# Moving the adaLN products of a two-layer diffusion backbone from TensorE to GpSimd

## The chip, the cores and the metric

One core of a Trainium2 chip runs the whole forward pass. The metric is device time of one execution in microseconds, as the median of several runs. The engines are TensorE (PE in the rows, PEld for its weight loads), VectorE (DVE), ScalarE (ACT), GpSimd (POOL) and SyncE (SP), which only issues DMAs. Each engine takes its own instructions in order and waits on semaphores for the others.

## The reference

Two layers, 256 latent tokens and 256 context tokens of width 1024 in float32. Each layer first turns a conditioning vector into six modulation vectors of 1024 (adaLN):

```python
mod_x = [m[:, None, :] for m in jnp.split(silu_c @ ada_w[i] + ada_b[i], 6, axis=-1)]
mod_c = jnp.split(silu_cc @ ada_w[i] + ada_b[i], 6, axis=-1)
hx = _modulate(_rms(x, norm1_w[i]), mod_x[0], mod_x[1])
y_x, y_c = _mixer(hx @ w_in[i], hc @ w_in[i], ...)
x = x + mod_x[2] * (y_x @ w_out[i])
x = x + mod_x[5] * ffn(_modulate(_rms(x, norm2_w[i]), mod_x[3], mod_x[4]))
```

`mod_x` (one column, from `c`) is for the latent tokens and `mod_c` (a second column, from `c_ctx`) for the context. Vectors 0 and 1 are shift and scale ahead of the mixer, 2 is the gate behind it, 3 and 4 are shift and scale ahead of the FFN, 5 is its gate. The mixer is an mLSTM with attention beside it; the FFN is a dense SwiGLU in layer 0 and eight experts with two chosen per token in layer 1. Layer 1 updates no context behind its mixer, so its vectors 2 to 5 need one column only.

## The kernel before

The weights of the dense products stream through `raw` tiles of 128x1024. Each is split into a high and a low float32r part (ScalarE line 143, VectorE line 144), and `mm3` (lines 328 to 331) makes one product of three matmuls. `gemm` (335) runs units of 128 output columns over 8 or 11 contraction tiles and yields after each unit. `mixer` (382) weaves four generators by a small clock (`STEPS`, line 39): the projections that are left, the mLSTM heads, the attention, and `extra`, the adaLN work. `ffn` (822) is a generator of four `gemm` calls. `bridge` (796) runs the end of a projection into the norm and the start of the next stage. At the end come the router and `experts`, whose weights are prefetched by SP into 16 buffers.

The adaLN products are made by `ada` (187). One part is two of the six vectors, 8 MB of weights in eight steps of 1 MB. For the first part of layer 0 this runs ahead of the first mixer, and this part stays as it is. The other five parts run through `adas` (228) as `extra` of a mixer: (0,1), (0,2) and (1,0) in mixer 0; (1,1) and (1,2) in mixer 1. One step loads two tiles `araw` of 512 KB by SP and makes eight matmuls `ada` with 32 columns of `cz` as weights (line 208; `cz` holds the SiLU of both conditioning vectors); after eight steps `sums` copies the row out, transposes it (217), and VectorE adds up four groups and the bias (220, 222).

Emission sets what each engine is given, but the framework reorders instructions within an engine when it builds the program, by its own estimates of when operands are ready. A pool's tile with one buffer makes the next writer wait for the last reader.

POOL has little to do: it clears `kz`, `akz` and `va` at the start of each mixer (417 to 422), clears `qkv` and `qkr` in `qk_norm` (642 to 655), multiplies the query and key tiles by the cosine table (678), clears `zb` (978), and issues two DMAs (962, 1285). In layer 1 `g2p` (970) spreads the gate of vector 5 over the partitions, for the experts; it stands among the products of the output projection.

Of the kernel before, what the change touches and what calls it, by code (L numbers as in the profile page):

```python
# [9 lines left out]
F32 = mybir.dt.float32  # L10
# [4 lines left out]
ALU = mybir.AluOpType  # L15
# [4 lines left out]
KT = 8  # L20
# [4 lines left out]
FCUT = 24  # L25
FE = 3584
NE = 8
BIG = 1e30
NRAW = 2
NWH = 5  # L30
UB = 4
EB = 2
# [13 lines left out]
HEAD = 3  # L46
# [3 lines left out]
TAILD = 3  # L50
# [18 lines left out]
def tile_hybrid(ctx: ExitStack, tc, a, tap=None):  # L69
# [155 lines left out]

        return load, products, sums

    def adas(pool, *parts):
        todo = [(*f, k) for f in [ada(l, p, pool, "araw", 2, 2) for l, p in parts] for k in range(KT)]
        todo[0][0](0)  # L230
        for i, (_, products, sums, k) in enumerate(todo):
            if k == 0:
                o = ps("ax", name="ada")
            products(o, k, k, k == 0, k == KT - 1)
            if i + 1 < len(todo):
                todo[i + 1][0](todo[i + 1][3])
            yield
            if k == KT - 1:
                sums(o, range(KT))
                yield  # L240

    def mod(layer, i, j):

# [138 lines left out]
    def mixer(layer, pool, extra):  # L382
# [253 lines left out]
        def qk_norm():  # L636

            dve.tensor_scalar(qwl, qw[:, layer:layer + 1], 0.125, None, op0=ALU.mult)
            w = PA.tile([128, TOK], F32, tag="sc", name="qkv", bufs=4)
            if not full:  # L640
                act.activation(w[0:32, 0:256], ssq[0][0:32, 0:256], AF.Copy)
                nc.gpsimd.memset(w[32:64, 0:256], 0.0)
                nc.gpsimd.memset(w[64:128, 0:256], 0.0)
            act.activation(w[:, q0:], ssq[0][:, q0:], AF.Copy)
            pt = ps("ax", name="qkT")
            for t in range(4):
                pe.transpose(pt[:, t * 128:(t + 1) * 128], w[:, t * 128:(t + 1) * 128], ident)
            v = tile("qv", [128, 64])
            r = tile("qr", [128, 64])
            view = lambda z: z.rearrange("p (t g r) -> p t g r", t=4, g=4)  # L650
            dve.tensor_scalar(view(v), view(pt)[:, :, :, 0:4], 1.0 / 64, EPS, op0=ALU.mult, op1=ALU.add)
            rsqrt(M, v, r, "q")
            yield
            w2 = PA.tile([128, TOK], F32, tag="sc", name="qkr", bufs=4)
            nc.gpsimd.memset(w2, 0.0)
            dve.tensor_copy(view(w2)[:, :, :, 0:4], view(r))
            pt = ps("ax", name="qkr")
            for t in range(4):
                pe.transpose(pt[:, t * 128:(t + 1) * 128], w2[:, t * 128:(t + 1) * 128], ident)
            rh = PA.tile([128, TOK], F32R, tag="sc", name="rh", bufs=4)  # L660
            rl = PA.tile([128, TOK], F32R, tag="sc", name="rl", bufs=4)
            act.activation(rh, pt, AF.Copy)
            dve.tensor_sub(rl, pt, rh)
            rot = cs[:, C_ROT - 128:C_ROT - 128 + 128]
            yield
            for i in (4, 0, 1, 2, 3):
                lo = 0 if i == 4 else q0
                b = ps("ax", name="qb")
                pe.matmul(b[:, lo:], qsel[:, i, :], rh[:, lo:], start=True, stop=False)
                pe.matmul(b[:, lo:], qsel[:, i, :], rl[:, lo:], start=False, stop=True)  # L670
                wc = kw[:, layer:layer + 1] if i == 4 else qwl
                z = qa[i]
                dve.scalar_tensor_tensor(z[:, lo:], z[:, lo:], wc, b[:, lo:], op0=ALU.mult, op1=ALU.mult)
                rp = ps("ax", name="rp")
                pe.matmul(rp[:, 0:256], rot, z[:, 256:512], start=True, stop=True)
                u = PA.tile([128, TOK], F32, tag="sc", name="u", bufs=4)
                dve.tensor_mul(u[:, 0:256], rp[:, 0:256], cs[:, C_SIN - 128:C_SIN - 128 + 256])
                nc.gpsimd.tensor_mul(u[:, 256:512], z[:, 256:512], cs[:, C_COS - 128:C_COS - 128 + 256])
                if i == 4:
                    for hv in range(2):  # L680
                        rr = slice(64 * hv, 64 * hv + 64)
                        dve.tensor_add(akz[hv][rr, 256:512], u[rr, 0:256], u[rr, 256:512])
                        act.activation(akz[hv][rr, 0:256], z[rr, 0:256], AF.Copy)
                else:
                    dve.tensor_add(z[:, 256:512], u[:, 0:256], u[:, 256:512])
                yield
# [135 lines left out]
    def ffn(acc):  # L822
        with tc.tile_pool(name="ff", bufs=1, reuse_waits="tile") as FF:
            f_rhs = [[], []]
            hold = {}

            def evac(key, o, *_):
                kind, m = key
                if kind == "g":
                    s = PA.tile([128, TOK], F32, tag="sc", name="sg", bufs=4)  # L830
                    act.activation(s, o, AF.Silu)
                    hold[m] = s
                    return
                f = PA.tile([128, TOK], F32, tag="sc", name="f", bufs=4)
                dve.tensor_mul(f, o, hold.pop(m))
                H = FF.tile([128, TOK], F32R, tag="fh", name="fh", bufs=15)
                L = FF.tile([128, TOK], F32R, tag="fl", name="fl", bufs=15)
                act.activation(H, f, AF.Copy)
                dve.tensor_sub(L, f, H)
                f_rhs[m // 11].append((H, L))  # L840

            def evac_d(key, o, lo, hi):
                half, m = key
                add_gated(0, 5, m, o, lo, hi)
                if half == 1:
                    if m == 0:
                        acc.append(new_acc())
                    square_add(acc[0], m, lo, hi)

            gu = [(0, (n, m)) for m in range(NFF) for n in ("g", "u")]  # L850
            down = lambda i: [(0, (i, m)) for m in range(KT)]
            yield from gemm(gu[:FCUT], hp, evac, KT, head=HEAD, halves=True)
            yield from gemm(down(0), f_rhs[0], evac_d, 11)
            yield from gemm(gu[FCUT:], hp, evac, KT)
            yield from gemm(down(1), f_rhs[1], evac_d, 11, head=HEAD, tail=TAILD)


    a0, mx = ExitStack(), ExitStack()
# [21 lines left out]
    S = Stats(acc)  # L880
    S.sums(0, TOK)
    M0 = mixer_pool("mix0", a0)
    g = mixer(0, M0, adas(lambda: mx.pool, (0, 1), (0, 2), (1, 0)))
    A = new_coef()
    def products0(k):
        o = ps("ax", name="ada")
# [27 lines left out]
    g = ffn(acc2)  # L914
    bridge(p, TAIL, acc, 0, 1, g)

    p, g = g, mixer(1, mixer_pool("mix1"), adas(lambda: mx.pool, (1, 1), (1, 2)))
    bridge(p, TAILD, acc2, 1, 0, g)
    run(g)
    mx.close()  # L920
# [444 lines left out]
def layout(i):  # L1365
# [10 lines left out]
    for h in range(4):  # L1376
# [9 lines left out]
    o["consts"] = np.ascontiguousarray(c[:, 128:])  # L1386
    o["ada"] = np.ascontiguousarray(i["ada_w"].reshape(2, 8, 128, 3, 2, 8, 128).transpose(0, 3, 5, 2, 1, 4, 6)
                                    ).reshape(2, 3, 8, 128, 2048)
    un = _units()
    win = np.zeros((2, 1024, NU * 128), np.float32)  # L1390
    for n, u in enumerate(UNITS):
# [43 lines left out]
```

## Time and profile before

| | |
|---|---|
| median of 3 runs | 1835.87 us (1835.19 to 1839.09) |
| the profiled execution | 1834.92 us, span of its trace 1833.2 us |
| mean granted TensorE clock | 0.988 of full |
| TensorE busy | 1724.5 us, 94% |
| VectorE busy | 586.9 us, 32% |
| ScalarE busy | 443.8 us, 24% |
| GpSimd busy | 19.6 us, 1% |
| HBM read | 469.36 MB, 257 GB/s over the span |

The stages, read off the lines at work: mixer 0 with its projections up to about 317 us, the FFN to about 700, mixer 1 and its output projection to 900, the router to 940, the experts to the end. A row of the profile names the line of the kernel, the engine, the operation, and the tiles as output<-input. float32 matmuls appear as two records each, float32r ones as one. "Idle before" is the time in which the engine had nothing to run ahead of that instruction, with what ended it. Matmul ends are modelled, so the durations of neighbours overlap; the step from start to start is the better measure.

### The profile page before, as it was taken

What the parts mean: (1) busy time and instruction counts of PE and PEld (TensorE: products, weight loads), DVE (VectorE), ACT (ScalarE), POOL (GpSimd) and SP (SyncE); (2) the same over time, 40 slices, a digit from 0 to 9 for tenths busy, and PEclk for the clock granted to TensorE, in tenths of its full rate; (3) what the DMA queues carried; (4) which work ended last, traced back from release to release, by engine and by line L of the source; (5) the groups of instructions that cost most, each with busy time, mean ns of one, the idle gap of its engine ahead of it and who ended that gap; (6) DMA issues with size and microseconds to landing.
All of it is one profiled execution on the core that took longest, in us unless ns stands there. A gap on an engine that the chain in (4) does not pass through costs nothing. (4 is left out here: it accounts for less than half of the span.)

```text
span 1833.2 us, 30457 instructions
## 1 busy us (share of the span) xinstructions
PE 1724.5 (94%) x13016; PEld 976.3 (53%) x13016; DVE 586.9 (32%) x1341; ACT 443.8 (24%) x852; POOL 19.6 (1%) x43
## 2 busy tenths in 40 slices
PE   6999899999999999999979999998988899999995
PEld 4866458888888889765734333333322233333331
DVE  6635565633333348465410200202020200211103
ACT  4543553432122225544311000101001000000001
POOL 1001000000000000000000000000000000000000
PEclk9999999999999999999989999999999999999997
DMA  8435541333333324465869999999999999999970
GB/s 314 148 122 182 181 160 58 99 97 95 101 92 93 103 70 137 140 196 160 326 255 417 416 418 399 361 417 416 418 416 417 417 416 418 403 408 357 339 305 24
DMA packets 84856, 472.65 MB, mean 258 GB/s; under 512 B 9424, under 2 KB 9808, under 8 KB 69088
## 3 DMA queue, kind: packets, MB, share of 16 engines
q1 hardware_dynamic: 84240, 469.36, 67.0%
q8 instruction: 118, 1.93, 0.4%
q0 software_dynamic: 176, 0.56, 0.1%
q10 hardware_dynamic: 288, 0.52, 0.1%
q14 instruction: 34, 0.28, 0.0%
HBM read 469.36 MB, written 1.05 MB: 257 GB/s over the span
## 5 line engine op out<-in xcount | busy, mean ns | idle before, releaser
L1145 PE MATMUL up<-rawe,G 128*32 128x448 f32 x5120 | 509.7, 543 | 19.0 <-PEq L1129 7.2
L1145 PEld LDWEIGHTS up<-rawe,G 128*32 128x32 f32 x5120 | 165.4, 110 | 339.0 <-issue 292.3
L329 PE MATMUL mm<-hh,wh 128*128 128x512 f32 (+1 forms) x856 | 305.4, 360 | 4.2 <-ACT hh L324 4.0
L330 PE MATMUL mm<-hl,wh 128*128 128x512 f32 (+1 forms) x856 | 304.4, 356 | 0.0
L331 PE MATMUL mm<-hh,wl 128*128 128x512 f32 (+1 forms) x856 | 303.4, 355 | 0.0
L1170 PE MATMUL y<-rawe,e 128*32 128x512 f32 x2240 | 252.4, 594 | 6.6 <-DMA rawe<-in_md_dram 3.3
L143 ACT ACTIVATE wh<-raw 128x1024 fp32r<-128x1024 f32 x120 | 127.1, 1059 | 329.8 <-PE mm L330 293.6
L144 DVE TENSOR_TENSOR wl<-raw,wh 128x1024 fp32r<-128x1024 f32 x120 | 146.7, 1223 | 176.9 <-ACT wh L143 174.4
L329 PEld LDWEIGHTS mm<-hh,wh 128*128 128x128 f32 x856 | 161.0, 189 | 31.1 <-ACT hh L324 5.4
L330 PEld LDWEIGHTS mm<-hl,wh 128*128 128x128 f32 x856 | 161.8, 189 | 27.3 <-issue 5.2
L331 PEld LDWEIGHTS mm<-hh,wl 128*128 128x128 f32 x856 | 161.7, 189 | 23.6 <-issue 1.6
L1210 DVE TENSOR_TENSOR hid<-sg,up 128x448 f32<-128x448 f32 x48 | 27.1, 617 | 424.7 <-PE up L1145 424.7
L1170 PEld LDWEIGHTS y<-rawe,e 128*32 128x32 f32 x2240 | 72.6, 109 | 162.9 <-issue 148.5
L1102 DVE TENSOR_TENSOR ye<-y,yc 32x512 f32<-32x512 f32 x48 | 32.7, 682 | 202.5 <-ACT yc L1100 201.8
L1191 ACT ACTIVATE e<-hT 128x384 f32<-128x384 f32 x48 | 23.4, 490 | 290.3 <-PE hT L1190 289.7
L329 PE MATMUL mm<-fh,wh 128*128 128x512 f32 (+1 forms) x209 | 75.3, 360 | 0.0
L330 PE MATMUL mm<-fl,wh 128*128 128x512 f32 (+1 forms) x209 | 75.1, 359 | 0.0
L331 PE MATMUL mm<-fh,wl 128*128 128x512 f32 (+1 forms) x209 | 75.1, 359 | 0.0
L1206 ACT ACTIVATE sg<-up 128x448 f32<-128x448 f32 x48 | 22.8, 544 | 209.5 <-PE up L1145 209.5
L208 PE MATMUL ada<-araw,cz 128*32 128x256 f32 x640 | 54.2, 390 | 13.6 <-DMA araw<-in_ada_dram 13.4
L1100 ACT ACTIVATE yc<-y 64x512 f32<-64x512 f32 x24 | 14.2, 593 | 207.6 <-PE y L1170 202.5
L330 PEld LDWEIGHTS mm<-fl,wh 128*128 128x128 f32 x209 | 39.3, 188 | 6.6
(265 smaller groups left out, 1362.5 us busy)
## 6 DMA issues: line engine op xcount, KB each, us to landing
rawe<-in_mg_dram SPq DMA_DIRECT2D x128, 896.0 KB, 17.5
rawe<-in_mu_dram SPq DMA_DIRECT2D x128, 896.0 KB, 17.3
rawe<-in_md_dram SPq DMA_DIRECT2D x112, 1024.0 KB, 17.0
raw<-in_ws_dram SPq DMA_DIRECT2D x120, 512.0 KB, 3.6
araw<-in_ada_dram SPq DMA_DIRECT2D x80, 512.0 KB, 4.4
a<-in_ada_dram SPq DMA_DIRECT2D x8, 1024.0 KB, 11.6
xall<-in_xT_dram SPq DMA_DIRECT2D x2, 1024.0 KB, 6.3
fn<-in_fn_dram POOLq DMA_DIRECT2D x1, 512.0 KB, 5.1
```

Of the source, the lines that this page charges most:

```text
L143: act.activation(h, raw, AF.Copy)
L144: dve.tensor_sub(l, raw, h)
L208: pe.matmul(o[32 * g:32 * g + 32, 0:256], cz[:, kt, 16 - 2 * row:48 - 2 * row], t[:, z:z + 256], start=(first and kt < 4), stop=(last and ...
L329: pe.matmul(out, wh, hh, start=first, stop=False)
L330: pe.matmul(out, wh, hl, start=False, stop=False)
L331: pe.matmul(out, wl, hh, start=False, stop=last)
L1102: dve.tensor_add(ye[32 * s:32 * s + 32, n * 512:(n + 1) * 512], y[s][32 * n:32 * n + 32, :], yc[32 * n:32 * n + 32, :])
L1145: pe.matmul(o[s][32 * c:32 * c + 32, 0:SC], g[:, k, 32 * s:32 * s + 32], w[k][:, c * SC:(c + 1) * SC], start=(k == 0), stop=(k == KT - 1), ...
L1170: pe.matmul(y[s][r:r + 32, :], e[s][:, 2 * i + par, :], w[i - lo][:, par * 1024 + n * 512:par * 1024 + (n + 1) * 512], start=(i == 0), sto ...
L1191: act.activation(e[s][:, 12 * st:12 * st + 12, :], pt[:, 0:384].rearrange("p (q c) -> p q c", c=32), AF.Copy)
L1206: act.activation(sg[s], o[:, 0:SC], AF.Silu)
L1210: dve.tensor_mul(hid[st, s], sg[s], o[:, 0:SC])
```

## The change

All vectors but the first two of layer 0 are now made on GpSimd. For each half of a vector (512 outputs) POOL itself issues eight DMAs of 256 KB, from the weights in a new layout `adb`. For each of the eight tiles it multiplies by one value of `cz` per partition and adds into an accumulator `au0` or `au1`, once for each column that is needed. TensorE then sums each accumulator over the partitions with a vector of ones, four matmuls of 128x1 per accumulator. VectorE adds the bias. Vectors (0,2) to (0,4) run beside mixer 0; (0,5), (1,0) and (1,1) beside the FFN, one step after each yield; (1,2) to (1,5), one column each, beside mixer 1. The weight tiles `araw` have two buffers in the mixers and four in the FFN; the accumulators and `af` have one each. The cosine multiplication goes from POOL to VectorE.

```diff
+EXTRA = 1
...
-    def adas(pool, *parts):
-        todo = [(*f, k) for f in [ada(l, p, pool, "araw", 2, 2) for l, p in parts] for k in range(KT)]
-        todo[0][0](0)
-        for i, (_, products, sums, k) in enumerate(todo):
-            if k == 0:
-                o = ps("ax", name="ada")
-            products(o, k, k, k == 0, k == KT - 1)
-            if i + 1 < len(todo):
-                todo[i + 1][0](todo[i + 1][3])
-            yield
-            if k == KT - 1:
-                sums(o, range(KT))
-                yield
+    def adas(pool, bufs, *vectors):
...
+        for layer, i in vectors:
+            nj = 1 if layer and i > 1 else 2
+            if (layer, i // 2) not in mods:
+                mods[layer, i // 2] = P1.tile([128, 16, 2], F32, name=f"mod{layer}{i // 2}")
+            for n in range(2):
+                z = slice(i % 2 * 8 + 4 * n, i % 2 * 8 + 4 * n + 4)
+                u = [pool().tile([128, 512], F32, tag=f"au{j}", name=f"au{j}", bufs=1) for j in range(nj)]
+                for k in range(KT):
+                    t = pool().tile([128, 512], F32, tag="araw", name="araw", bufs=bufs)
+                    nc.gpsimd.dma_start(t, a["adb"][layer, i, n, k])
+                    for j in reversed(range(nj)):
+                        c = cz[:, k, 16 + j:17 + j]
+                        if k == 0:
+                            nc.gpsimd.tensor_scalar(u[j], t, c, None, op0=ALU.mult)
+                            continue
+                        f = pool().tile([128, 512], F32, tag="af", name="af", bufs=1) if j else t
+                        nc.gpsimd.tensor_scalar(f, t, c, None, op0=ALU.mult)
+                        nc.gpsimd.tensor_tensor(u[j], u[j], f, ALU.add)
+                    if k % 2:
+                        yield
+                o = ps("ax", name="adas")
+                for j in range(nj):
+                    for k in range(4):
+                        pe.matmul(o[:, k * nj + j:k * nj + j + 1], u[j][:, k * 128:(k + 1) * 128], ones,
+                                  start=True, stop=True)
+                bias = adab[:, layer, i // 2 * 16 + z.start:i // 2 * 16 + z.stop]
+                dve.tensor_add(mods[layer, i // 2][:, z, 0:nj], o[:, 0:4 * nj].rearrange("p (k j) -> p k j", j=nj),
+                               bias.unsqueeze(2).to_broadcast([128, 4, nj]))
...
-                nc.gpsimd.tensor_mul(u[:, 256:512], z[:, 256:512], cs[:, C_COS - 128:C_COS - 128 + 256])
+                dve.tensor_mul(u[:, 256:512], z[:, 256:512], cs[:, C_COS - 128:C_COS - 128 + 256])
...
-            yield from gemm(gu[:FCUT], hp, evac, KT, head=HEAD, halves=True)
-            yield from gemm(down(0), f_rhs[0], evac_d, 11)
-            yield from gemm(gu[FCUT:], hp, evac, KT)
-            yield from gemm(down(1), f_rhs[1], evac_d, 11, head=HEAD, tail=TAILD)
+            extra = adas(lambda: FF, 4, (0, 5), (1, 0), (1, 1))
+            for g in (gemm(gu[:FCUT], hp, evac, KT, head=HEAD, halves=True), gemm(down(0), f_rhs[0], evac_d, 11),
+                      gemm(gu[FCUT:], hp, evac, KT), gemm(down(1), f_rhs[1], evac_d, 11, head=HEAD, tail=TAILD)):
+                for mark in g:
+                    if mark == "tail":
+                        run(extra)
+                    yield mark
+                    step(extra, EXTRA)
...
-    g = mixer(0, M0, adas(lambda: mx.pool, (0, 1), (0, 2), (1, 0)))
+    g = mixer(0, M0, adas(lambda: mx.pool, 2, (0, 2), (0, 3), (0, 4)))
...
-    p, g = g, mixer(1, mixer_pool("mix1"), adas(lambda: mx.pool, (1, 1), (1, 2)))
+    p, g = g, mixer(1, mixer_pool("mix1"), adas(lambda: mx.pool, 2, *((1, i) for i in range(2, 6))))
```

The order of the instructions shows where the new work stands. Lines of the changed kernel are 20 to 24 higher than before in the same code (329 is 349, 970 is 994).

TensorE in the FFN, in a unit of the gate and up products. `mm` is the unit's output, `hh`/`hl` the high and low tokens, `wh`/`wl` the high and low weights. Before:

```order
L329 MATMUL mm<-hh_89,wh 128x512 [waits DVE_49]
L330 MATMUL mm<-hl_90,wh 128x512
L331 MATMUL mm<-hh_89,wl 128x512
L329 MATMUL mm<-hh_91,wh 128x512
L330 MATMUL mm<-hl_92,wh 128x512
L331 MATMUL mm<-hh_91,wl 128x512
```

And in the change, at the third of the six sums in the FFN:

```order
L349 MATMUL mm<-hh_91,wh 128x512
L350 MATMUL mm<-hl_92,wh 128x512
L351 MATMUL mm<-hh_91,wl 128x512
L256 MATMUL adas<-ones,au_3328 128x1 [waits Pool_49]
L256 MATMUL adas<-ones,au_3328 128x1 x3
L256 MATMUL adas<-ones,au_3329 128x1 x4
L349 MATMUL mm<-hh_93,wh 128x512
L350 MATMUL mm<-hl_94,wh 128x512
L351 MATMUL mm<-hh_93,wl 128x512
```

Eight sums now stand inside the unit, the first with a wait for POOL; the next such place is 85 products further on.

POOL at the same time, from one half-vector to the next. Before, POOL had nothing in the FFN; its neighbours there were the last cosine product of mixer 0 and the first memsets of mixer 1:

```order
L678 TENSOR_TENSOR u<-qa_510,cs 128x256 [waits DVE_49,Pool_49]
L678 TENSOR_TENSOR u<-qa_511,cs 128x256 [waits DVE_49,Pool_49]
L417 MEMSET kz_5745 64x512 [waits DVE_49,PE_49,Pool_49]
L417 MEMSET kz_5746 64x512
L417 MEMSET kz_5747 64x512
```

In the change (`au_3329` and `au_3328` are the accumulators of one half-vector, `au_3430` and `au_3429` those of the next):

```order
L249 TENSOR_SCALAR af<-araw,cz 128x512 [waits DMASW2_49,Pool_49]
L250 TENSOR_TENSOR au_3328<-au_3328,araw 128x512 [waits Pool_49]
L249 TENSOR_SCALAR araw<-araw,cz 128x512 [waits Pool_49]
L246 TENSOR_SCALAR au_3430<-araw,cz 128x512 [waits DMASW1_49,PE_49]
L246 TENSOR_SCALAR au_3429<-araw,cz 128x512 [waits Pool_49]
L250 TENSOR_TENSOR au_3430<-au_3430,af 128x512 [waits Pool_49]
L250 TENSOR_TENSOR au_3429<-au_3429,araw 128x512 [waits Pool_49]
L242 DMA araw<-in_adb_dram 128x512 x3
```

The product that opens the new accumulator waits for TensorE, which has to have read the old one; the last add of the old half-vector and two products of the new one's second tile stand in front of it.

TensorE at the end of mixer 1's output projection. Before, the router's sum of squares `ss` followed the last product at once, and `g2p` stood further up among the products:

```order
L329 MATMUL mm<-hh_103,wh 128x256
L330 MATMUL mm<-hl_104,wh 128x256
L331 MATMUL mm<-hh_103,wl 128x256
L286 MATMUL ss<-ones,acc 128x1 [waits DVE_49,PE_49]
L286 MATMUL ss<-ones,acc 128x1
```

In the change (`au_7786`, `au_7824` and `au_7862` are the last three half-vectors, of (1,4) and (1,5)):

```order
L351 MATMUL mm<-hh_103,wl 128x256
L256 MATMUL adas<-ones,au_7786 128x1 [waits PE_49,Pool_49]
L256 MATMUL adas<-ones,au_7786 128x1 x3
L256 MATMUL adas<-ones,au_7824 128x1 [waits PE_49,Pool_49]
L256 MATMUL adas<-ones,au_7824 128x1 x3
L256 MATMUL adas<-ones,au_7862 128x1 [waits PE_49,Pool_49]
L256 MATMUL adas<-ones,au_7862 128x1 x3
L994 MATMUL g2p<-sml,mod_7685 128x128 [waits DVE_49]
L994 MATMUL g2p<-sml,mod_7685 128x128 x3
L994 MATMUL g2p<-sml,mod_7685 128x128 [waits DVE_49]
L994 MATMUL g2p<-sml,mod_7685 128x128 x3
L306 MATMUL ss<-ones,acc 128x1 [waits PE_49]
```

Three sums with a wait for POOL and all of `g2p` now stand between the last product and the router.

## Rows read from the trace of the kernel before

**Rows 1.** The page, part 1: busy time, share of the span, instructions.

```profile
PE 1724.5 (94%) x13016; PEld 976.3 (53%) x13016; DVE 586.9 (32%) x1341; ACT 443.8 (24%) x852; POOL 19.6 (1%) x43
```

**Rows 2.** Windows by stage: length, busy time of each engine, granted clock, DMA, GB/s.

```profile
core 0: us, PE busy (x) PEld busy (x) DVE busy (x) ACT busy (x) POOL busy (x), PEclk, DMA share, GB/s
...
144.00:262.00 118.00, 112.04 (x738) 64.13 (x737) 71.39 (x228) 60.18 (x172) 4.96 (x5) 1.00 0.55 180
...
317.00:700.00 383.00, 380.84 (x1890) 321.91 (x1889) 156.33 (x248) 114.74 (x152) 3.26 (x10) 1.00 0.31 95
...
784.00:880.00 96.00, 89.41 (x635) 57.43 (x634) 57.97 (x191) 47.49 (x114) 4.31 (x6) 0.98 0.51 162
...
900.00:940.00 40.00, 28.65 (x192) 16.76 (x194) 13.12 (x58) 9.30 (x21) 0.58 (x1) 0.83 0.55 213
940.00:1833.00 893.00, 831.05 (x7852) 294.02 (x7844) 125.60 (x228) 79.58 (x151) 0.00 (x0) 0.98 0.94 379
```

**Rows 3.** The page, part 5: the products that the change removes.

```profile
L208 PE MATMUL ada<-araw,cz 128*32 128x256 f32 x640 | 54.2, 390 | 13.6 <-DMA araw<-in_ada_dram 13.4
```

**Rows 4.** POOL by line, shapes apart: busy us, mean ns; its last memset by time.

```profile
L678 POOL TENSOR_TENSOR u<-qa,cs 128x256 f32<-128x256 f32 x8 | 6.4, 797 | 19.3 <-DVE qa L673 10.8 <-DVE rd L607 3.6 <-DVE mod L222 2.7
...
L678 POOL TENSOR_TENSOR u<-ka,cs 128x256 f32<-128x256 f32 x2 | 2.4, 1180 | 63.0 <-DVE ka L673 63.0
...
L655 POOL MEMSET qkr<- 128x512 f32 x2 | 1.1, 527 | 96.0 <-PE ssq L470 91.0 <-ACT E L576 5.0
L962 POOL DMA_DIRECT2D wr<-in_router_dram x1 | 0.7, 697 | 0.8 <-POOLq L1425 0.8
L1285 POOL DMA_DIRECT2D fn<-in_fn_dram x1 | 0.6, 580 | 35.9 <-PE tT L1021 35.9
...
L422 POOL MEMSET va<- 128x4 f32 x8 | 0.4, 98 | 0.0
...
L976 POOL COPY wr<-wr 128x64 f32<-128x64 f32 x1 | 0.2, 237 | 4.7 <-DMA wr<-in_router_dram 4.7
...
41.41 0.20 POOL L422 MEMSET va<- 128x4 f32 x4
```

**Rows 5.** Line 678 alone: duration in ns, least, median and most.

```profile
L678 POOL TENSOR_TENSOR u<-qa,cs x8: 726/750/1148, 169.5 to 820.1; 128x256 f32<-128x256 f32 x8
```

**Rows 6.** Timeline of TensorE's weight loads at a 128x1 product: start us, us.

```profile
317.48 0.53 PEld L286 LDWEIGHTS ss<-ones,acc 128*128 128x128 f32 x4
...
317.93 0.19 PEld L329 LDWEIGHTS mm<-hh,wh 128*128 128x128 f32 x1
```

**Rows 7.** Timeline of TensorE: the products next to which the sums now stand.

```profile
144.24 0.39 PE L569 MATMUL U<-mask,identb 128*128 128x512 bf16 x1
...
262.17 1.12 PE L709 MATMUL sc<-akz,qa 128*128 128x512 f32 x2
...
331.74 0.28 PE L331 MATMUL mm<-hh,wl 128*128 128x256 f32 x1
...
425.19 0.39 PE L329 MATMUL mm<-hh,wh 128*128 128x512 f32 x1
...
784.40 0.39 PE L331 MATMUL mm<-hh,wl 128*128 128x512 f32 x1
...
900.21 0.28 PE L331 MATMUL mm<-hh,wl 128*128 128x256 f32 x1
```

**Rows 8.** Windows of the removed products (`ada`) alone: length, PE busy.

```profile
100.00:144.00 44.00, 6.33 (x64) 1.92 (x64) 0.00 (x0) 0.00 (x0) 1.00 0.43 144
...
262.00:275.00 13.00, 2.16 (x32) 0.47 (x24) 0.48 (x2) 0.39 (x1) 1.00 0.25 82
700.00:784.00 84.00, 4.26 (x56) 1.20 (x56) 0.00 (x0) 0.00 (x0) 1.00 0.43 141
```

**Rows 9.** DMA issues by POOL: KB each, median us from issue to landing.

```profile
fn<-in_fn_dram POOLq DMA_DIRECT2D x1, 512.0 KB, 5.1
...
wr<-in_router_dram POOLq DMA_DIRECT2D x1, 32.0 KB, 5.6
```

More of the change, by code (lines that the diff above doesn't have):

```diff
@@ L1388, in layout @@
                                     ).reshape(2, 3, 8, 128, 2048)
+    o["adb"] = np.ascontiguousarray(i["ada_w"].reshape(2, 8, 128, 6, 2, 512).transpose(0, 3, 4, 1, 2, 5))
+    o["ada"] = np.ascontiguousarray(o["ada"][:1, :1])
     un = _units()
```

## The prediction

> **What bounds the kernel now.** I read the page's shares first. TensorE is busy 94% of the span and GpSimd (POOL) 1% [rows 1], so moving work from the one to the other looks free. The stage windows say where a change can act [rows 2]. From 940 us on the expert weights stream at 379 GB/s with the DMA engines 94% busy; nothing there is touched. Between 900 and 940 us, while routing is worked out, they are only 55% busy: their buffers are full and wait for TensorE. So whatever moves the start of the experts, early or late, moves the end by as much. In the FFN TensorE is busy 380.8 of 383 us, in the two mixers 112.0 of 118 and 89.4 of 96. What the change takes out is one group: 54.2 us busy, with 13.6 us idle in front of it, in which the weights were still on their way [rows 3]; together 67.8 us, or 1.25 us for each busy one. POOL today runs a few instructions [rows 4]. I read them last, and they decide.
>
> **What TensorE saves.** It loses the 67.8 us. It gains the sums: 12 two-column half-vectors of 8 matmuls and 8 one-column ones of 4, 128 matmuls, each two records: 256. The nearest row is `ss`, the same shape: 4 records take the weight path from 317.48 to 317.93, 0.113 us each [rows 6]. That is 1.8 us for a two-column half-vector, 0.9 for a one-column one, 29 us in all. TensorE's saving is at most 67.8 - 29 = 39 us, if it never waits.
>
> **What POOL gets.** A two-column half-vector issues 8 DMAs, 16 TENSOR_SCALARs and 14 TENSOR_TENSOR adds, all 128x512; a one-column one 8, 8 and 7. None stands in the trace at this size, so each is bounded.
> - DMA issue: 0.697 and 0.580 us [rows 4]. I take 0.64.
> - TENSOR_SCALAR: not under MEMSET 128x512, 0.527, which reads nothing. Above, by COPY: 237 ns for 64 elements, less the 98 ns of the smallest MEMSET, is 2.17 ns each, so 1.21 us for 512. I take 0.75, nearer to the row of the right size.
> - TENSOR_TENSOR: 128x256 takes 726 ns at least, 750 in the median [rows 5]. Doubling all but a fixed 237 ns (a whole COPY) gives 1.22 us from the least, doubling all but 98 ns gives 1.40 from the median. I take 1.33. In the mixers the ten of them mean 874 ns [rows 4], 1.165 times the median, because VectorE is busy beside them: 1.55 there, at most 1.63.
>
> The accumulators have one buffer, so the first product of a half-vector waits until TensorE has summed the one before, as POOL's order shows. POOL and TensorE therefore run in a cycle: POOL's work, then the sums. I add 1.8 us for these and 1.0 for waits of POOL on its own results (0.9 and 0.5 for one column), which no row shows. **One cycle**: FFN 16 x 0.75 + 14 x 1.33 + 8 x 0.64 + 2.8 = 38.5 us (30.9 to 47.4); mixer 0 the same with 1.55, 41.6 us (30.9 to 50.6); mixer 1 8 x 0.75 + 7 x 1.55 + 8 x 0.64 + 1.4 = 23.4 us (18.2 to 28.1). The low ends take the shortest rows and half of the sums as covered.
>
> The Trainium skill speaks against this change (GPSIMD Engine Reference, section 4.1): elementwise work belongs on VectorE, and two-input operations are about twice as slow on GpSimd. Its section 3.1 times an add of 2048 elements at 4497 ns; a quarter, 1.12 us, as an estimate by that page, would make the FFN's cycle 35.6 us and its term below 85 instead of 99. No run here shows that size.
>
> **What waits.** TensorE takes its instructions in order. A sum that POOL hasn't finished holds back every product behind it: projections, scores, FFN. Idle POOL time elsewhere is worth nothing; what counts is how far apart the sums stand. I place them by the product in front of each, in the trace of before [rows 7].
> - *Mixer 0.* The first sum stands behind the mask product at 144.24, which ends by 144.6. Of that, 6.33 us busy since 100 us are products that go [rows 8], with their idle 7.9, so TensorE arrives at 137. POOL can start behind the memsets at about 41.6 us [rows 4] and has long finished; but then it waits for this sum. Five cycles later, at 137 + 208 = 345, comes the sixth sum. TensorE stood at that place, among the last score products, at 262. That is +83, less 2.7 for the products removed after 262 [rows 8]: **+80 us** (+26 to +125).
> - *FFN.* First and sixth sum stand at 331.74 and 425.19, 93.5 us apart, 18.7 a cycle. The first I cost at nothing: 67 us lie between it and the mixer's last sum, and one POOL pass needs 36; if the FFN's buffers came free over 30 us late, it would show. Five cycles of 38.5 take 192.5: **+99 us** (+61 to +144). Nothing can be won back, TensorE being full on either side.
> - *Mixer 1.* The first sum stands at 784.40, less 4.26 x 1.25: 779. Seven cycles later is 943. The last three sums stand behind the whole output projection, whose last product started at 900.21: **+42 us** (+6 to +76).
> - *Behind it* the eight `g2p` products, which stood inside the projection, now wait for the last sum: 16 records, **+2 us**.
>
> Costed at nothing: VectorE's ten rope multiplications, at most 0.8 us each by POOL's rows and beside the waits above; the removed row copies and reductions; SP, rid of 80 issues with none behind them that is late; POOL's own memsets for `qkr` and `qkv`, now queued behind products, since they come before the sum that holds TensorE anyway. If POOL were fast these memsets would be next to show, because query and key normalisation wait for them. TensorE's clock fell to a granted 0.83 in the stage with waits [rows 2]; a lower level inside a cycle would be hidden, as TensorE needs half of it.
>
> **Sum**: 80 + 99 + 42 + 2 = +223 us. The profiled execution took 1834.9 us (span 1833.2), 1.0 below the median of 1835.87: 1834.9 + 223 = **2058 us**. Low ends together: +95, 1930 us. High ends together: +346, 2181 us; that all four prices are at their high end is unlikely, so I stop at 2140.
>
> **The rivals.**
> - *Faster: POOL keeps up and TensorE never waits.* The point is in the FFN: a cycle under 18.7 us. Then the saving on TensorE is whole, and the time 1835 - 39 = 1796. For it: POOL is idle 99% of the span, and the order places the sums as if about 19 us were enough. Against it: 38 instructions in 18.7 us is 0.49 each, under even the MEMSET's 0.527, while an add of half the size takes 0.726. Chance 0.04.
> - *Prices mostly fixed per instruction.* If 128x512 adds cost 0.80, little more than 128x256, and products 0.527, a two-column cycle is 25 us. Then mixer 0 loses nothing, the FFN 33 us, and mixer 1 gains up to 14, for it is TensorE's again: 1835 + 20, so 1815 to 1930. For it: MEMSET 128x4 at 98 ns says no, COPY at 237 ns for 64 elements says perhaps. Chance 0.10, of which 0.02 within 0.2%.
> - *POOL and VectorE block each other, or the loads come late.* `ka`'s multiplication took 1180 ns in the mean against 797 for `qa` [rows 4]. If every add were so stretched, 2.1 us, a two-column cycle would be 49 us, with the one-column at 27: 1835 + 117 + 152 + 68 + 2 = 2174. In mixer 1 there are two load buffers; POOL's two DMAs landed after 5.6 and 5.1 us [rows 9], and a round of landing, product and add, 5.3 + 2.3, covers two tiles: 3.8 us a tile against 2.9 by POOL's work, 51 us more over seven cycles. Chance 0.10. The Trainium skill (SBUF — State Buffer, section "Who interferes with whom") says that a VectorE instruction with two SBUF inputs and a GpSimd one that reads SBUF exclude each other for whole instructions; the stretched rows agree with it.
> - *The change does less than it says.* TensorE's 54.2 us could hardly shrink if the sums were dear; at 0.113 us a record they are not. Folded into the forecast.
>
> **How the numbers follow.** My forecast, a POOL-paced kernel between 1930 and 2140, has 0.76; above it 0.10, below it 0.14 in two cases. Range 1930 to 2140, nearly 8 in 10. About 0.2% (3.7 us) is what a measurement of this kernel tells from no change: faster 0.04, same 0.02, slower 0.94.
>
> **What would show it.** POOL busy for some 500 us (256 products x 0.75 and 224 adds x 1.4); the idle time before the sums' line on TensorE, released by POOL, of 180 us or more; sums in the FFN 38 us apart instead of 19; the expert stage as long as before and some 220 us later. A POOL add near 0.8 us, or sums without idle time before them, would make the forecast wrong; so would idle time that VectorE or a DMA ends instead.

## The result and the profile after

The changed kernel takes **2282.03 us** (median of four runs, 2276.1 to 2282.66) against 1835.53 us before: a ratio of 1.2426, 95% interval 1.2399 to 1.2453. The forecast was 2058 us, 1930 to 2140. The direction and the mechanism held, the size did not: the rise is 447 us where 223 were forecast. The profiled execution has a span of 2280.7 us, 447.5 more than before.

Busy times of the page, where [rows 1] had 19.6 us for POOL:

```profile
PE 1773.1 (78%) x12622; PEld 1045.4 (46%) x12622; DVE 658.8 (29%) x1361; ACT 439.4 (19%) x845; POOL 824.6 (36%) x673
```

Windows by stage, columns as in [rows 2]:

```profile
139.00:262.00 123.00, 68.82 (x310) 50.45 (x309) 49.67 (x127) 32.90 (x88) 104.57 (x83) 0.76 0.20 58
262.00:400.00 138.00, 50.75 (x226) 33.88 (x226) 41.78 (x109) 26.74 (x83) 125.62 (x101) 0.67 0.14 40
500.00:745.00 245.00, 110.63 (x461) 92.49 (x461) 42.15 (x43) 28.29 (x37) 228.69 (x177) 0.69 0.23 73
500.00:800.00 300.00, 165.63 (x695) 138.08 (x696) 59.63 (x66) 41.77 (x53) 230.44 (x180) 0.74 0.24 75
800.00:1115.00 315.00, 306.77 (x1596) 259.87 (x1595) 144.83 (x240) 106.71 (x160) 38.70 (x35) 0.99 0.32 101
1115.00:1345.00 230.00, 112.53 (x632) 88.44 (x630) 81.09 (x216) 47.79 (x118) 186.38 (x159) 0.72 0.25 77
1300.00:1345.00 45.00, 2.45 (x11) 2.37 (x11) 0.16 (x1) 0.00 (x0) 39.34 (x35) 0.50 0.21 64
1390.00:2280.00 890.00, 830.35 (x7812) 291.67 (x7805) 125.51 (x228) 79.24 (x151) 0.00 (x0) 0.98 0.94 379
```

The experts take 890 us and move 379 GB/s, as before; they only start later. In mixer 0 POOL is full (125.62 of 138 us) and TensorE is not (50.75). So it is in the middle of the FFN: from 500 us to the last sum at 745, POOL is busy for 228.69 of 245 us, TensorE for 110.63. In mixer 1, from 1115 to 1345 us, it is 186.38 and 112.53 of 230 us. Between 800 and 1115 us, with the new work of the FFN done, it is the other way round. The groups of the page that replace [rows 3], and behind them TensorE's largest waits (us in total, times, longest):

```profile
L256 PE MATMUL adas<-ones,au 128*128 128x1 f32 x256 | 53.4, 336 | 367.9 <-POOL au L250 367.9
L249 POOL TENSOR_SCALAR araw<-araw,cz 128x512 f32<-128x512 f32 x140 | 235.8, 1684 | 22.9 <-DMA araw<-in_adb_dram 20.8
L250 POOL TENSOR_TENSOR au<-au,araw 128x512 f32<-128x512 f32 x140 | 184.8, 1320 | 7.2
```

```profile
PE adas L256 <- POOL au L250: 367.9, 17, 31.8
PE ss L306 <- DVE acc L273: 14.0, 2, 13.7
```

TensorE loses 367.9 us in 17 waits, all for POOL's last add ahead of a sum. Nothing else comes near. Least, median and most of POOL's two operations, in ns:

```profile
L249 POOL TENSOR_SCALAR araw<-araw,cz x140: 1552/1564/3057, 53.4 to 1341.5; 128x512 f32<-128x512 f32 x140
L250 POOL TENSOR_TENSOR au<-au,araw x140: 1249/1265/2336, 55.1 to 1343.1; 128x512 f32<-128x512 f32 x140
```

The add is where it was put (1.33 us taken, 1.265 measured). The product, costed at 0.75 us with an upper bound of 1.21, takes 1.56: more than the add, which has one input more. POOL does nothing else in these stretches; a piece of its timeline (start us, us):

```profile
383.38 1.27 POOL L250 TENSOR_TENSOR au<-au,af 128x512 f32<-128x512 f32 x1
384.62 1.56 POOL L249 TENSOR_SCALAR araw<-araw,cz 128x512 f32<-128x512 f32 x1
386.27 1.26 POOL L250 TENSOR_TENSOR au<-au,araw 128x512 f32<-128x512 f32 x1
387.82 0.59 POOL L242 DMA_DIRECT2D araw<-in_adb_dram  x1 [0.30 <-POOL au L250]
388.46 1.57 POOL L249 TENSOR_SCALAR af<-araw,cz 128x512 f32<-128x512 f32 x1
```

TensorE's sums in the FFN; what stands in brackets is the idle time before them:

```profile
487.83 1.84 PE L256 MATMUL adas<-ones,au 128*128 128x1 f32 x16
536.68 3.57 PE L256 MATMUL adas<-ones,au 128*128 128x1 f32 x16 [21.03 <-POOL au L250]
591.00 3.57 PE L256 MATMUL adas<-ones,au 128*128 128x1 f32 x16 [29.84 <-POOL au L250]
641.68 3.58 PE L256 MATMUL adas<-ones,au 128*128 128x1 f32 x16 [26.06 <-POOL au L250]
694.58 3.57 PE L256 MATMUL adas<-ones,au 128*128 128x1 f32 x16 [28.01 <-POOL au L250]
744.67 3.57 PE L256 MATMUL adas<-ones,au 128*128 128x1 f32 x16 [25.55 <-POOL au L250]
```

The first finds POOL done, as forecast. The others are 51.4 us apart, not 38.5. And after a wait the same 16 records take 3.57 us, not 1.84: TensorE comes back at its lower clock. The clock granted over each of these five sums is 0.50, the 1.2 GHz level, and over the first it is 1.00.

Starts of the sums in this and the later runs, in us (for the kernel before: the places of [rows 7]). They split every difference into stages:

| kernel | sixth sum, mixer 0 | first, FFN | sixth, FFN | first, mixer 1 | last, mixer 1 | span |
|---|---|---|---|---|---|---|
| before (places) | 262.2 | 331.7 | 425.2 | 784.4 | 900.2 | 1833.2 |
| the change | 406.3 | 487.8 | 744.7 | 1115.4 | 1344.4 | 2280.7 |
| constant factor | 402.1 | 482.3 | 731.9 | 1101.7 | 1322.3 | 2253.5 |
| two-input product | 380.6 | 473.1 | 701.9 | 1076.1 | 1274.4 | 2206.8 |
| products on ScalarE | 321.3 | 398.1 | 535.7 | 919.2 | 1096.1 | 2033.1 |
| spread in the FFN | 408.4 | 493.7 | 838.3 | 983.3 | 1212.5 | 2149.0 |
| two accumulators | 407.0 | 489.4 | 726.5 | 1118.5 | 1348.0 | 2281.0 |
| loads by SyncE | 394.7 | 489.3 | 717.7 | 1113.7 | 1294.3 | 2229.3 |
| four buffers, mixer 1 | 407.3 | 488.4 | 743.6 | 1114.5 | 1308.4 | 2243.0 |
| VectorE, same places | 269.7 | 341.0 | 435.3 | 824.6 | 977.9 | 1907.7 |

For the change: mixer 0 +144 us, the stretch to the FFN's first sum +12, the FFN's five cycles +163, the stretch to mixer 1 +11.5, its seven cycles +113, the end +3.3: 447 us.

### The profile page after: what moved, and what is told of

Read it like the earlier page. It is cut to its first block, busy times and chain, and to the rows that moved or that the text cites. A ratio compares the mean times of both kernels' runs of the same rounds, so it can differ in the third digit from the quotient of the medians.

```text
span 2280.7 us, 30201 instructions
## 1 busy us (share of the span) xinstructions
PE 1773.1 (78%) x12622; PEld 1045.4 (46%) x12622; DVE 658.8 (29%) x1361; ACT 439.4 (19%) x845; POOL 824.6 (36%) x673
## 5 line engine op out<-in xcount | busy, mean ns | idle before, releaser
L256 PE MATMUL adas<-ones,au 128*128 128x1 f32 x256 | 53.4, 336 | 367.9 <-POOL au L250 367.9
L350 PE MATMUL mm<-hl,wh 128*128 128x512 f32 (+1 forms) x856 | 313.8, 367 | 5.9 <-DVE hl L345 5.9
L349 PE MATMUL mm<-hh,wh 128*128 128x512 f32 (+1 forms) x856 | 314.7, 371 | 4.1 <-ACT hh L344 4.0
L351 PE MATMUL mm<-hh,wl 128*128 128x512 f32 (+1 forms) x856 | 314.0, 367 | 0.0
L249 POOL TENSOR_SCALAR araw<-araw,cz 128x512 f32<-128x512 f32 x140 | 235.8, 1684 | 22.9 <-DMA araw<-in_adb_dram 20.8
L256 PEld LDWEIGHTS adas<-ones,au 128*128 128x128 f32 x256 | 52.2, 308 | 374.8 <-POOL au L250 374.8
L250 POOL TENSOR_TENSOR au<-au,araw 128x512 f32<-128x512 f32 x140 | 184.8, 1320 | 7.2
L249 POOL TENSOR_SCALAR af<-araw,cz 128x512 f32<-128x512 f32 x84 | 141.7, 1687 | 18.7 <-DMA araw<-in_adb_dram 17.9
L250 POOL TENSOR_TENSOR au<-au,af 128x512 f32<-128x512 f32 x84 | 114.2, 1360 | 2.7
L242 POOL DMA_DIRECT2D araw<-in_adb_dram x160 | 92.2, 577 | 43.8 <-DVE rd L628 19.5
```

The costliest lines, as they stand in the source:

```text
L242: nc.gpsimd.dma_start(t, a["adb"][layer, i, n, k])
L249: nc.gpsimd.tensor_scalar(f, t, c, None, op0=ALU.mult)
L250: nc.gpsimd.tensor_tensor(u[j], u[j], f, ALU.add)
L256: pe.matmul(o[:, k * nj + j:k * nj + j + 1], u[j][:, k * 128:(k + 1) * 128], ones, start=True, stop=True)
L349: pe.matmul(out, wh, hh, start=first, stop=False)
L350: pe.matmul(out, wh, hl, start=False, stop=False)
```

## The experiments

The theory: POOL's instructions between two sums set the time, and the product is dearer than costed. The rivals: its operand (a factor read from SBUF), the turn-taking on one accumulator, the loads, VectorE in POOL's way, or the places of the sums.

### Is it the factor from SBUF?

```diff
-nc.gpsimd.tensor_scalar(u[j], t, c, None, op0=ALU.mult)
+nc.gpsimd.tensor_scalar(u[j], t, 0.5, None, op0=ALU.mult)
...
-nc.gpsimd.tensor_scalar(f, t, c, None, op0=ALU.mult)
+nc.gpsimd.tensor_scalar(f, t, 0.5, None, op0=ALU.mult)
```

> The products on GpSimd are made with the constant 0.5 and not with a value per partition; loads, sums and places stay. Left out: the conditioning factor, so the modulation vectors are other numbers. Theory A (GpSimd's work between two sums sets the time, and the multiplication is dear because it reads its factor from SBUF): the multiplication falls from 1.56 us to some 0.75 us, a cycle of a half-vector with two columns from 52 to about 39 us, one with one column from 33 to about 26; over 5 + 5 + 7 cycles that is about 65 + 65 + 45 = 175 us, so near 2105 us. Theory B (a one-input multiplication of 128x512 takes 1.56 us whatever its factor is): 2282 us as before.

Measured: 2255.46 us in one run (the kernel before took 1831.33 us on the chip of this run and the next three, 4 us less than beside the change).

```profile
L249 POOL TENSOR_SCALAR araw<-araw 128x512 f32<-128x512 f32 x140 | 223.4, 1596 | 21.5 <-DMA araw<-in_adb_dram 19.8
```

The product falls by some 0.09 us, from a mean of 1684 ns to 1596, not to 0.75. The operand's source is not the cause: POOL takes about 1.5 us for a one-input multiplication of this size either way. Theory B, but for those 27 us.

### The same product as a two-input operation

```diff
-nc.gpsimd.tensor_scalar(u[j], t, c, None, op0=ALU.mult)
+nc.gpsimd.tensor_tensor(u[j], t, c.to_broadcast([128, 512]), ALU.mult)
...
-nc.gpsimd.tensor_scalar(f, t, c, None, op0=ALU.mult)
+nc.gpsimd.tensor_tensor(f, t, c.to_broadcast([128, 512]), ALU.mult)
```

> The products on GpSimd are made by the two-input operation, with the value per partition spread by a stride of zero as the second input. Theory A (GpSimd's price of an operation with a value per partition is its own, above that of the two-input operation): a product falls from 1.56 to the 1.27 us of the adds, 4.7 us less in a cycle with two columns and 2.3 us with one, over 5 + 5 + 7 cycles 63 us: near 2220 us. Theory B (a product is dear because it reads a tile that a transfer has just written, or because VectorE or a transfer hinders it): it stays at 1.56 us or more, and the time stays at 2282 us.

Measured: 2208.76 us in one run.

```profile
L249 POOL TENSOR_TENSOR araw<-araw,cz x140: 1028/1044/1915, 50.7 to 1272.0; 128x512 f32<-128x512 f32 x140
```

Theory A, and by more than expected: with its second input at a stride of zero the two-input product takes 1.04 us, under the add's 1.27 and two thirds of the one-input product's 1.56. So TENSOR_SCALAR itself is dear on POOL. Cycles fall from 52.6 to 44.4 us in mixer 0, 8.2 for 16 products of 0.52 us less. Some of it is lost again: mixer 0 begins later (first sum at 158.71 us, not 143.18), and from its sixth sum to the first of the FFN it is 92.5 us instead of 81.5. VectorE and TensorE in that stretch:

```profile
405.48 18.11 DVE L644 TENSOR_SCALAR hs<-hs,hr 128x128 f32<-128x128 f32 x4
...
423.65 0.47 PE L648 MATMUL hT<-sml,hs 128*128 128x128 f32 x1 [15.41 <-DVE hs L644]
```

Four small operations of VectorE last 18.11 us, until POOL turns to a DMA issue at 423.46, and TensorE waits 15.41 us for them. The same happens in the FFN's first cycle, which takes 50.4 us where the other four take 44.6 in the mean. VectorE, POOL (around the end) and TensorE there:

```profile
481.70 15.83 DVE L289 SCALAR_TENSOR_TENSOR r<-rst,rsy 128x2 f32<-128x2 f32 x1
...
495.26 1.25 POOL L250 TENSOR_TENSOR au<-au,af 128x512 f32<-128x512 f32 x1
496.48 1.03 POOL L249 TENSOR_TENSOR araw<-araw,cz 128x512 f32<-128x512 f32 x1
497.46 0.58 POOL L242 DMA_DIRECT2D araw<-in_adb_dram  x1
...
497.59 1.22 PE L315 MATMUL rbc<-sml,r 128*128 128x128 f32 x4 [19.46 <-DVE r L289]
```

An operation of VectorE on 128x2, 0.16 us elsewhere, lasts 15.83 us. POOL runs two-input operations without a gap all that time; VectorE's ends at 497.53, when POOL turns to an issue at 497.46. TensorE waits 19.46 us for the value. All four operations of VectorE that last over 9 us in this run end within 1.2 us of a break in POOL's row, an issue or a wait. In the change, where TENSOR_SCALARs stand between the adds, no operation of VectorE lasts over 4.3 us. The Trainium skill (SBUF — State Buffer, section "Who interferes with whom") says that the two engines hold the shared port for a whole instruction; here VectorE stayed out for a row of them, so the measurement goes further than the page.

### Products on ScalarE

```diff
-nc.gpsimd.tensor_scalar(u[j], t, c, None, op0=ALU.mult)
+act.activation(u[j], t, AF.Copy, scale=c)
...
-nc.gpsimd.tensor_scalar(f, t, c, None, op0=ALU.mult)
+act.activation(f, t, AF.Copy, scale=c)
```

> The products are made on ScalarE with the value per partition as its scale; GpSimd issues the loads and adds. Theory A (GpSimd's instructions between two sums set the time): a cycle with two columns is then 14 adds of 1.27 us, 8 issues of 0.59 us and 2 to 3.6 us for the sums, about 26 us, one with one column about 15 to 20 us; mixer 0 gets 5 x 26 = 130 us for the 119 us that the places stood apart before, the FFN 130 for 93, mixer 1 7 x 18 = 126 for 116: some 60 us over 1835, so 1880 to 1940 us. Theory B (the waits are those of the weight loads, of TensorE's clock or of the one accumulator, and GpSimd's speed matters little): over 2100 us.

Measured: 2034.86 us in one run: 247 us of the loss gone, but 95 above theory A's range.

```profile
L249 ACT ACTIVATE araw<-araw,cz 128x512 f32<-128x512 f32 x140 | 100.3, 717 | 63.2 <-DMA araw<-in_adb_dram 61.2 <-POOL au L250 0.7
```

The FFN's cycle is 27.5 us, near the expected 26. The mixers' are not: 33.6 for 26, and 25.3 for 15 to 20. In mixer 1 ScalarE waits for loads (55.4 us of the 61.2), which two buffers don't hide. In mixer 0 POOL no longer sets the pace: TensorE waits for one sum there, 4.9 us, and 38.5 us for values of the heads and the attention that ScalarE and VectorE make, at a granted clock of 0.81. And 24 us appear where none were expected, between the FFN's last sum and mixer 1: 383.4 us for 359.2. The section on two accumulators and SyncE's loads takes that up.

### Spreading the sums in the FFN

```diff
+            n = [0, 0.0]
...
-                    step(extra, EXTRA)
+                    n[0] += 1
+                    n[1] += 1.0 if n[0] <= 16 else 5.4
+                    while n[1] >= 13.0:
+                        n[1] -= 13.0
+                        step(extra, EXTRA)
```

> In the FFN a step of the new work stands every 13 us of TensorE's work, not after every yield, so that the six sums stand some 52 us apart over the whole FFN; mixers as in the change. Theory A (in the FFN only the places of the sums are wrong, GpSimd has the time by the end of the stage): the five waits of 21 + 30 + 26 + 28 + 25.5 us = 131 us go or shrink to a few us, and the clock in the FFN comes back: 2130 to 2170 us. Theory B (GpSimd's work hinders TensorE or VectorE whatever its place, or the sums wait at the later places too): within 30 us of 2282 us.

Measured: 2151.0 us in one run, theory A. Two of the sums in the timeline, and the window of the FFN from 490 to 840 us:

```profile
791.81 1.84 PE L256 MATMUL adas<-ones,au 128*128 128x1 f32 x16
838.27 3.57 PE L256 MATMUL adas<-ones,au 128*128 128x1 f32 x16 [20.11 <-POOL au L250]
```

```profile
490.00:840.00 350.00, 327.20 (x1523) 272.40 (x1521) 141.83 (x148) 89.87 (x111) 257.80 (x188) 0.97 0.37 116
```

Four of the five waits are gone and one of 20.11 us is left: 130.5 - 20.1 = 110 us. The time fell by 131. So some 20 us more come with the waits: the sums are back at 1.84 us and the granted clock at 0.97, where it was 0.74 between 500 and 800 us. POOL does the same work at nearly the same prices (a product 1736 ns in the mean, for 1684), and it costs much less where its results are asked for late: from the FFN's first sum to mixer 1's it is 489.6 us, 37 more than before, of which the last wait is 20.1 and the sums themselves are 12.8.

### Two accumulators; loads by SyncE

```diff
-name=f"au{j}", bufs=1)
+name=f"au{j}", bufs=2 if bufs == 4 else 1)
```

> In the FFN the accumulators get two buffers each, so that GpSimd need not wait for a sum before it starts the next half-vector; mixers as in the change. Theory A (GpSimd's own instructions set the cycle, and the one accumulator adds only the time of eight sums): the cycle in the FFN falls from 51.4 to some 48 us, 5 x 3.5 = 18 us: 2255 to 2270 us. Theory B (that TensorE and GpSimd wait for each other in turn is what makes the cycle long): more than 60 us less, under 2220 us.

```diff
-                    nc.gpsimd.dma_start(t, a["adb"][layer, i, n, k])
+                    nc.sync.dma_start(t, a["adb"][layer, i, n, k])
```

> SyncE issues the loads of the new weights, not GpSimd. Theory A (each of GpSimd's issues costs its 0.58 us in the cycle): 4.6 us less in every cycle, in mixer 1 up to 6, since its loads no longer wait for GpSimd's turn; 23 + 23 + 32 to 42 us: 2190 to 2205 us. Theory B (the loads then stand in SyncE's order ahead of the projections' weights and hold these up while they wait for a buffer): GpSimd's cycle falls as well, but TensorE waits for weights instead, and the time stays within 30 us of 2282 us or rises.

Measured: 2281.48 us (ratio to before 1.2431, interval 1.2401 to 1.2461) and 2232.86 us (1.2166, 1.2136 to 1.2197). Both shorten POOL's cycle as theory A said: 47.4 us in the FFN with two accumulators, 45.7 with SyncE's loads, for 51.4. With two accumulators nothing of that arrives at the end, with SyncE's loads only what mixer 1 gains (cycle 25.8 for 32.7, 48 us). SyncE's loads also bring the sixth sum of mixer 0 11.6 us earlier, but up to the FFN's first sum these are gone: TensorE waits 11.1 and 8.1 us there for values of VectorE.

The table says where the rest went: the FFN's last sum comes 18 and 27 us earlier, but from there to mixer 1 it takes 392 and 396 us instead of 371. TensorE is busy for 384.4 and 390.2 of these. It has more left to do. Matmuls `mm` between the six sums of the FFN, counted in the built programs' order:

| kernel | between sums 1 and 2, ... 5 and 6 | in all |
|---|---|---|
| the change | 116, 85, 85, 85, 80 | 451 |
| two accumulators | 27, 89, 81, 85, 81 | 363 |
| loads by SyncE | 93, 60, 59, 56, 59 | 327 |
| products on ScalarE | 112, 65, 68, 66, 64 | 375 |
| VectorE, same places | 114, 33, 4, 68, 96 | 315 |

The framework puts a sum where it thinks that it will be ready; with a quicker accumulation by its estimate it puts the sums closer. 88 and 124 products fewer at some 0.216 us (1715 of them fill most of the 370.7 us behind the FFN's sums) are 19 and 27 us, about what the shorter cycles gained; the 76 fewer with products on ScalarE are 16 of its 24 us. This refutes the assumption under both expectations, that the places stay. With SyncE's loads mixer 0 also begins 20 us later (first sum at 163.66, not 143.18): up to that sum ScalarE waits 38.8 us for weights, as theory B had it, and 7.3 us in the change; TensorE waits 20.9 us for ScalarE's `vf`, and 3.9 in the change.

### Load buffers in mixer 1

```diff
-adas(lambda: mx.pool, 2, *((1, i) for i in range(2, 6)))
+adas(lambda: mx.pool, 4, *((1, i) for i in range(2, 6)))
```

> In mixer 1 the new weights get four load buffers for two; nothing else. Theory A (in mixer 1, too, GpSimd's instructions set the cycle, and its waits for loads, about 5 of the 32.7 us, are on top): the seven cycles fall to some 28 us, 7 x 4.7 = 33 us: 2245 to 2260 us. The last three sums stand at the end of mixer 1 whatever happens, so the gain isn't given back by their places. Theory B (with more buffers GpSimd only waits for TensorE instead): 2275 us or more.

Measured: 2244.93 us in one run (before, on the same chip, 1836.25): theory A, 37 us. The cycle is (1308.4 - 1114.5) / 7 = 27.7 us for 32.7. Here a shorter cycle pays in full, since the last sums stand behind the whole output projection: the last two in this run, the last three in the change.

### VectorE accumulates, in the same places

```diff
-                        f = pool().tile([128, 512], F32, tag="af", name="af", bufs=1) if j else t
-                        nc.gpsimd.tensor_scalar(f, t, c, None, op0=ALU.mult)
-                        nc.gpsimd.tensor_tensor(u[j], u[j], f, ALU.add)
...
+                        dve.scalar_tensor_tensor(u[j], t, c, u[j], op0=ALU.mult, op1=ALU.add)
```

> The change with its places and GpSimd's loads, but VectorE makes each product and its add in one instruction of about 0.72 us. Theory A (only the speed of the engine that accumulates made the change slow): a cycle with two columns is 16 x 0.72 + 2 = 14 us by VectorE, under the 18.7 us between sums in the FFN; in the mixers the two load buffers set it, about 2.5 us a tile, 20 us a half-vector, which fits mixer 0 (5 x 20 against 119 us) and misses mixer 1 by some 24 us (7 x 20 against 116): 1835 - 39 + 24, so 1800 to 1840 us. Theory B (VectorE waits in its order for loads that come late and holds up the low parts of the weights, so TensorE waits there): over 1860 us.

Measured: 1913.76 us, ratio 1.0432 (1.0414 to 1.0449); neither theory's range, and TensorE hardly waits for the weights' low parts (4.1 us in the FFN). VectorE's group, and the window from the FFN's first sum on:

```profile
L248 DVE SCALAR_TENSOR_TENSOR au<-araw,cz,au 128x512 f32<-128x512 f32 x224 | 159.5, 745 | 27.1 <-DMA araw<-in_adb_dram 26.7
```

```profile
330.00:430.00 100.00, 81.17 (x455) 70.48 (x455) 85.61 (x160) 26.80 (x40) 20.88 (x39) 0.88 0.50 148
```

One instruction of 0.745 us does what took POOL 2.8. That is 368 of the change's 446 us. The other 78 have two places. Mixer 1 takes 153 us for its seven cycles, 38 more than before (21.9 us each, 20 expected). VectorE waits 27.2 us for loads there, with two buffers; four were not tried with it. In the FFN the framework did not keep the places, and the sums are drawn so close that all of VectorE's work falls into 100 us, of which it is busy for 85.61; TensorE is idle for 19 of them, and from the FFN's first sum to mixer 1's it is 483.6 us for 452.7.

### Only layer 1, beside the FFN, with room

Mixer 0 as in the kernel before, nothing in mixer 1. Loads by SyncE two tiles ahead, a step every 7.2 us:

```diff
+PACE = 7.2
...
-            extra = adas(lambda: FF, 4, (0, 5), (1, 0), (1, 1))
+            extra = adas(lambda: FF, 4, *((1, i) for i in range(6)))
...
-    g = mixer(0, M0, adas(lambda: mx.pool, 2, (0, 2), (0, 3), (0, 4)))
+    g = mixer(0, M0, adas_pe(lambda: mx.pool, (0, 1), (0, 2)))
...
-    p, g = g, mixer(1, mixer_pool("mix1"), adas(lambda: mx.pool, 2, *((1, i) for i in range(2, 6))))
+    p, g = g, mixer(1, mixer_pool("mix1"), iter(()))
```

with products on ScalarE and adds on POOL in the first run, and VectorE's one instruction in the second.

> Layer 0 as in the kernel before: its two other parts are made on TensorE in mixer 0. The six vectors of layer 1 are made beside the FFN alone, a step of two weight tiles every 7.2 us of TensorE's work: products on ScalarE, adds on GpSimd, loads by SyncE two tiles ahead. Theory A (what made the change slow is that GpSimd's work did not fit between the places of the sums, and nothing else): the adds are 4 x 14 + 8 x 7 = 112 of 1.27 us, 142 us in a stage of 380 us, so no sum waits; TensorE gives up three parts and makes 128 sums of 0.11 us, and nothing else of its own grows: 15 to 30 us under the kernel before, 1805 to 1820 us. Theory B (GpSimd's or ScalarE's instructions beside the FFN hold up the splits and evictions that TensorE waits for, or its clock falls): 1840 us or more.

> As the run with layer 1 beside the FFN, but VectorE makes each product and its add in one instruction, and GpSimd does nothing of it. 128 such instructions of some 0.6 to 0.8 us (VectorE's operations on 128x512 in the FFN's rows) are 77 to 100 us in a stage in which VectorE is busy for less than half. Theory A (there is room beside the FFN): 1805 to 1820 us, as with ScalarE and GpSimd or a little below. Theory B (TensorE waits for the low parts of the weights that VectorE makes, line 144): 1830 us or more.

Measured: 1835.45 us, ratio 0.9990 (0.9973 to 1.0007), and **1822.00 us, ratio 0.9927 (0.9901 to 0.9953)**. The second is 0.7% faster than the kernel before. Both miss theory A's 1805 to 1820 us, the second by 2 us; the first lies between the two theories. The groups and the window of the FFN:

```profile
L278 PE MATMUL adas<-ones,au 128*128 128x1 f32 x128 | 14.9, 242 | 0.0
L272 DVE SCALAR_TENSOR_TENSOR au<-araw,cz,au 128x512 f32<-128x512 f32 x112 | 80.6, 748 | 2.0 <-DMA araw<-in_adb_dram 0.7
```

```profile
323.00:691.00 368.00, 368.00 (x1798) 309.74 (x1797) 206.33 (x305) 99.96 (x127) 1.56 (x3) 1.00 0.48 149
```

The sums never wait. TensorE is busy for all 368 us of the FFN, beside 206.33 of VectorE. Three parts at 67.8 / 5 = 13.6 us less 14.9 for the sums should give 26 us; 11.4 arrive in the span. Mixer 0 ends 6.3 us earlier for one part given up (the FFN's first `ss` at 311.3 us for 317.6), mixer 1 is 22.7 us shorter for two, the FFN 13.2 longer, the part behind mixer 1 4.4 longer. The run with ScalarE and POOL loses 8.4 us against it by the end of mixer 0 and 5.2 in the FFN; POOL's adds mean 1.47 to 1.52 us there. Which of its engines' waits these 13.6 us are was not tried.

## Why the prediction was wrong in size and right in kind

**Right.** Sums wait in TensorE's order for POOL, once per half-vector, with POOL running nearly back to back. The wait of "180 us or more" is 367.9; the experts are as long as before; the FFN's first sum costs nothing; the adds (1.33 taken, 1.265 measured in the median) and the issues (0.64, 0.59) hold. The 0.113 us for a record of a sum holds at the full clock (1.84 / 16).

**The step that failed** is the price of POOL's TENSOR_SCALAR, "I take 0.75", and its upper bound "by COPY", 1.21 us; 1.56 was measured. The bound took a slope from another operation, with a fixed part from a third, and I priced the one-input operation under the two-input one, though no row says that. The Trainium skill (GPSIMD Engine Reference, section 4.1) has one-input operations at roughly line rate on GpSimd and two-input ones about half as fast as on VectorE. The rows here agree with the second (1.265 us for the add, 0.69 for VectorE's TENSOR_TENSOR `rl<-qkr,rh` of this size) and not with the first (1.56 us, 0.48 for the same TENSOR_SCALAR on VectorE in the last run). With 1.56 my own cycles become 51.5, 54.6 and 29.9 us, the terms +164 (FFN), +145 (mixer 0) and +88 (mixer 1), and the time 1835 + 399 = 2234 us: 176 of the 224 us that were missing.

**The other 48.** Mixer 1's two load buffers cost 37 us; the rival named this mechanism, at 51 us, and gave it a tenth. "A lower level inside a cycle would be hidden" is half wrong. TensorE's products are hidden, but the sums stand in the cycle themselves, and 1.7 us more in each of ten cycles and 0.9 in seven are 23 us; the stretches behind a mixer and behind the FFN were 12 and 11.5 us longer. In the first of these the granted clock is 0.91, where it was 1.00, and TensorE waits 5.4 us for VectorE's `r`; in the second it waits 7.0 us for values of ScalarE and VectorE. Cheaper adds in the mixers than the 1.55 taken gave some of it back, since VectorE hardly stretched them there: 4 us in each cycle of mixer 0 and 2 in mixer 1.

**The rivals.** POOL does not keep up, and prices are not fixed per instruction. POOL and VectorE do hinder each other, but in the change most of this lay inside the waits for the sums: TensorE waits 367.9 us for POOL and 5.4 us for `r`, ahead of which VectorE's operations of 0.15 to 0.43 us took up to 2.07. It cost more, 15.4 and 19.5 us in a wait, where POOL's products were two-input operations as well. And "idle POOL time elsewhere is worth nothing" proved true in reverse: with the sums spread, POOL's work in the FFN cost 37 us in place of 175.

## What to carry to other kernels

Price an operation on an engine by a row of that very operation at that size; without one, let the range reach at least over the dearest neighbour, here the two-input add (taken at 1.33 us, still 0.23 too little). What a slow engine costs is not its busy time but the distance between the places where a faster one, in its own order, asks for a result: ask late, load ahead, and check where a scheduler puts the asking after every edit, since it may take back what a shorter cycle gives. An idle engine is no reason to use it: VectorE did product and add together in 0.745 us, POOL in 2.8.

## What the hardware showed unexpectedly

- On GpSimd, 128x512 float32: one-input product 1.56 us with a factor from SBUF, 1.49 with a constant (medians), two-input add 1.27, two-input product with one input at a stride of zero 1.04. Why the one-input form is dearest stays open.
- VectorE can be kept out by GpSimd for much longer than one instruction: a 128x2 operation of 0.16 us took 15.83 us beside an unbroken row of GpSimd's two-input operations, and ended when GpSimd turned to a DMA issue.
- TensorE came back from its waits for POOL in mixer 0 and the FFN at half the clock (0.50 granted): 3.57 us instead of 1.84 for the same sums, each of the ten times.
